# The Hyena inverses of a two-layer diffusion backbone with tokens in the rows, and the filter bias moved into the spectra

## The chip, the cores and the metric

The kernel runs on one core of one Trainium2 chip. The metric is the device time of one execution, in microseconds (us). An execution of the kernel before takes 2646.43 us (median of three). All matrix products read fp32r operands, split into a high and a low half, so that one product of two numbers is made of two or three passes on TensorE.

## The reference

Two layers over 256 latent tokens of width 2048. Layer 0 is a Mamba-2 group beside latent attention, layer 1 an order-2 Hyena long convolution, and each is followed by a SwiGLU FFN. The change lies in layer 1 (`d` is 2048, `gate` is the first and then the second third of the projection, `y` the last third):

```python
def long_conv_bidir(u, h_two):
    seq_len, d = u.shape[1], u.shape[2]
    k = jnp.concatenate([h_two[:, 0], jnp.zeros((1, d)), jnp.flip(h_two[1:, 1], axis=0)], axis=0)
    k = k / jnp.sum(jnp.abs(k), axis=0, keepdims=True)
    kf = jnp.fft.rfft(k, axis=0)
    uf = jnp.fft.rfft(u, n=2 * seq_len, axis=1)
    return jnp.fft.irfft(uf * kf, n=2 * seq_len, axis=1)[:, :seq_len]

# hyena():
proj = dwconv_centred(u @ w_in + b_in, short_w, short_b)
x1, x2, y = proj[..., :d], proj[..., d:2 * d], proj[..., 2 * d:]
for i, gate in enumerate((x1, x2)):
    h_two = jnp.einsum('lf,fkd->lkd', hid, fw_out[:, i]) * window[:, None, :]
    y = gate * (long_conv_bidir(y, h_two) + fbias[i] * y)
return y @ w_out + b_out
```

## The kernel before

**Stages.** A startup stage computes the first layer's modulation by matrix products (`on_pe`, tile `ps_mod`), the sums of squares of both inputs, and the spectra of the Hyena filters (`filters` and `spectra`). Then come layer 0, its output projection, the FFN of layer 0, layer 1 (`layer1`, from about 1446 us to about 1803 us), its output projection, the FFN of layer 1 and a final norm. Activations stand transposed: a row (partition) is a channel, a column a token.

**Weights.** `run` walks over a list of tasks, each with one 1 MB weight block. SP issues the load (`raw`), ScalarE (ACT) writes the high half (`whi`, L339), VectorE (DVE) the low half (`wlo`, L340), TensorE (PE) multiplies: `wide` sends the low weights against 256 columns (L562) and the high weights against 512 (L561, L564). Loads run two tasks ahead and the halves come from a ring of three buffers, so ACT and DVE wait for PE when they are ahead.

**Background steps.** After each task `run` ticks a queue of generators; `hyena_steps(g)` is one of them, for 8 groups `g` of 256 channels, and each runs twice (`o` = 0, 1). The emitted order is then placed by a scheduler for each engine, which fills the spaces between dependent steps with the products of the current task. Every engine works through its own list in order.

**Modulation.** 160 columns of modulation weights are multiplied on DVE (`mods_use`, L445, tile `mraw`), a few for each task at the rates in `MODS` (for layer 0's two parts, the FFN of layer 0, layer 1, the FFN of layer 1).

**Filters.** For each of 8 pieces (4 channel blocks, 2 orders) `filters` loads a weight tile `fwr` by POOL's queue, splits it (`fwh`, `fwl`), makes four products `pss`, multiplies by a window, splits, and sums absolute values in `am`. `spectra` transforms the piece (`psk`), adds and subtracts the two halves (`ko`), writes them to a scratch in HBM (`kscr`), and puts the inverse norm in `kinv`. The tags `fwr`, `fwh` and `fwl` have two buffers each.

**One convolution.** With channels in the rows, `y` is first transposed (`ps_yT`, L1263) so that tokens stand in the rows, even tokens apart from odd ones; it is split, transformed (`ps_u`, 12 products) and multiplied by the spectrum (`kf`). The result is split into `ph` and `pl`. The inverse (`ps_c`) takes `ph` and `pl` as the stationary operand and the inverse table `dih`, `dil` as the moving one, so its result has channels in the rows again: 2 halves of 4 frequency pieces of 3 products, 24 in all, each over 256 columns. Then bias, norm and gate are applied by one ACT and two DVE instructions for each half (L1300 to L1302).

Of the kernel before, what the change touches and what calls it, by code (L numbers as in the profile page):

```python
# [10 lines left out]
F32 = mybir.dt.float32  # L11
F32R = mybir.dt.float32r
AF = mybir.ActivationFunctionType
ALU = mybir.AluOpType
# [3 lines left out]
P = 128  # L18
D = 2048
S = 256  # L20
# [18 lines left out]
MODS = (1.8, 0.6, 0.68, 0.08, 0.6)  # L39
# [132 lines left out]
def _prepare(inputs):  # L172
    g = {k: np.asarray(v) for k, v in inputs.items()}
    f32 = np.float32
    a = {}
# [46 lines left out]
    w = g["ev_w_in"][0]  # L222
# [33 lines left out]
    fw = g["hy_fw_out"][0]  # L256
    a["fw"] = fw.transpose(1, 2, 0, 3).reshape(2, P, 4, 512).transpose(0, 2, 1, 3)
# [9 lines left out]
class _Kernel:  # L267
# [428 lines left out]
    def filters(self, pool):  # L696
        nc, a = self.nc, self.a
# [31 lines left out]
        yield  # L729
        wt = None  # L730
# [39 lines left out]
    def spectra(self, pool, fh, fl, gi, s2, am):  # L770

        nc = self.nc
        g, i = gi // 2, gi % 2
        for w in range(2):
            two = []
            for tt in (1, 0):
                ps = self.ps.tile([P, 512], F32, tag=("acc", "ms")[tt], name=self.nm("psk"), bufs=3)
                r = slice(w * P, (w + 1) * P)
                self.mm3(ps, (fh[:, tt, r], fl[:, tt, r]), (s2[w][0][:, tt], s2[w][1][:, tt]), True, True)
                two.append(ps)  # L780
# [470 lines left out]
    def hyena_steps(self, g):  # L1251
        nc, hp = self.nc, self.hyp
        y = self.hyt[g, 0]
        for o in range(2):
            kf = hp.tile([P, 4, S], F32, tag="kf", name=self.nm("kf"), bufs=1)
            src = self.kscr[2 * (g // 2) + o].rearrange("p (a b) -> p a b", b=512)
            nc.sync.dma_start(kf, src[:, :, (g % 2) * S:(g % 2) * S + S])
            yth = hp.tile([P, 2, S], F32R, tag="yth", name=self.nm("yth"), bufs=1)
            ytl = hp.tile([P, 2, S], F32R, tag="ytl", name=self.nm("ytl"), bufs=1)
            pst = self.ps.tile([P, 2, S], F32, tag="ms", name=self.nm("ps_yT"))  # L1260
            for tt in range(2):
                for c in range(2):
                    nc.tensor.transpose(pst[:, tt, c * P:(c + 1) * P], y[:, c, tt::2], self.mat("ident"))  # L1263
            self.split(yth, ytl, pst)
# [14 lines left out]
            for f2, u in enumerate((ev, odd)):  # L1279
# [10 lines left out]
            if g == 0 and o == 1:  # L1290
                self.mh, self.ml, self.mhl = self.pair("hmix")
            for c in range(2):
                ch = 2 * g + c
                psc = self.ps.tile([P, 512], F32, tag="ms", name=self.nm("ps_c"))
                cs = slice(c * P, (c + 1) * P)
# [7 lines left out]
                if o == 1:  # L1303
                    self.split(self.mh[:, ch, :S], self.ml[:, ch, :S], yc)
# [239 lines left out]
    def layer1(self):  # L1544
        nc, a, hp = self.nc, self.a, self.hyp
        self.hn = {}
# [66 lines left out]
```

## Time and profile before

| | |
|---|---|
| median of three runs | 2646.43 us (2644.79 to 2648.49) |
| the profiled execution | 2648.55 us, span of its instructions 2646.7 us |
| granted TensorE clock, mean of the span | 0.99 of full speed |
| PE busy | 2572.2 us, 97% |
| DVE busy | 2088.8 us, 79% |
| ACT busy | 1428.2 us, 54% |

Times in the rows count from the span's first instruction. A matmul's duration contains its way through the array, and successive ones overlap: what one costs a stream is the distance between two starts. The same holds, to a lesser degree, for DVE.

### The profile page before, as it was taken

What the parts mean: (1) busy time and instruction counts of PE and PEld (TensorE: products, weight loads), DVE (VectorE), ACT (ScalarE), POOL (GpSimd) and SP (SyncE); (2) the same over time, 40 slices, a digit from 0 to 9 for tenths busy, and PEclk for the clock granted to TensorE, in tenths of its full rate; (3) what the DMA queues carried; (4) which work ended last, traced back from release to release, by engine and by line L of the source; (5) the groups of instructions that cost most, each with busy time, mean ns of one, the idle gap of its engine ahead of it and who ended that gap; (6) DMA issues with size and microseconds to landing.
All of it is one profiled execution on the core that took longest, in us unless ns stands there. A gap on an engine that the chain in (4) does not pass through costs nothing.

```text
span 2646.7 us, 39320 instructions
## 1 busy us (share of the span) xinstructions
PE 2572.2 (97%) x15128; PEld 2200.9 (83%) x15128; DVE 2088.8 (79%) x3178; ACT 1428.2 (54%) x2298; POOL 7.4 (0%) x22
## 2 busy tenths in 40 slices
PE   5979999999999999999999999999999999999997
PEld 2548779887988888888888888888998888888886
DVE  7867878777898888888889999898887656656656
ACT  4544656646654544544556755556654544544455
POOL 0000000000000000000000000000000000000000
PEclk9979999999999999999999999999999999999999
DMA  9956557556588887988887555456587654545543
GB/s 354 342 211 221 189 186 278 208 203 234 215 323 310 335 310 284 343 308 298 330 302 271 198 179 180 170 184 235 207 313 261 217 178 169 215 171 195 192 162 125
DMA packets 105610, 635.58 MB, mean 240 GB/s; under 512 B 11344, under 2 KB 19920, under 8 KB 44624
## 3 DMA queue, kind: packets, MB, share of 16 engines
q1 hardware_dynamic: 101904, 620.49, 64.3%
q10 hardware_dynamic: 2304, 8.39, 0.8%
q0 software_dynamic: 1216, 4.20, 0.5%
q8 instruction: 119, 1.95, 0.3%
q14 instruction: 67, 0.55, 0.1%
HBM read 622.55 MB, written 10.49 MB: 239 GB/s over the span
## 4 chain that ended last, share of the span: by engine, by line
PE 92%; DVE 4%; ACT 1%; issue 1%; DMA 1%; SPq 0%; DVEq 0%; ACTq 0%
PE acc L561 41%; PE acc L562 23%; PE acc L819 7%; PE acc L564 3%; PE acc L372 3%; PE acc L373 3%; PE acc L374 3%; PE ps_mod L1383 1%; DVE wlo L340 1%; PE ps_c L372 1%; PE ps_c L374 1%; PE ps_c L373 1%; DVE mraw L445 1%; PE ps_y L1070 0%; PE ps_o L1201 0%
## 5 line engine op out<-in xcount | busy, mean ns | idle before, releaser
L561 PE MATMUL acc<-act,whi 128*128 128x512 f32 x3525 | 1255.6, 396 | 3.9 <-ACT whi L339 3.9
L340 DVE TENSOR_TENSOR wlo<-raw,whi 128x1024 fp32r<-128x1024 f32 (+1 forms) x842 | 938.7, 1119 | 239.1 <-ACT whi L339 232.8
L339 ACT ACTIVATE whi<-raw 128x1024 fp32r<-128x1024 f32 (+1 forms) x842 | 814.6, 972 | 469.7 <-PE acc L561 244.5
L562 PE MATMUL acc<-act,wlo 128*128 128x256 f32 x3760 | 1020.7, 281 | 1.4 <-DVE wlo L340 1.4
L561 PEld LDWEIGHTS acc<-act,whi 128*128 128x128 f32 x3525 | 666.2, 189 | 150.4 <-ACT whi L339 4.9
L562 PEld LDWEIGHTS acc<-act,wlo 128*128 128x128 f32 x3760 | 709.3, 189 | 23.1 <-DVE wlo L340 2.9
L561 PE MATMUL acc<-hh,whi 128*128 128x512 f32 x1280 | 456.4, 395 | 0.0
L445 DVE SCALAR_TENSOR_TENSOR mraw<-mraw,cb 128x2048 f32<-128x2048 f32 x160 | 365.8, 2287 | 30.7 <-DMA mraw<-in_mod 30.4
L562 PE MATMUL acc<-hh,wlo 128*128 128x256 f32 x1408 | 376.2, 282 | 0.0
L561 PEld LDWEIGHTS acc<-hh,whi 128*128 128x128 f32 x1280 | 240.9, 188 | 51.0
L562 PEld LDWEIGHTS acc<-hh,wlo 128*128 128x128 f32 x1408 | 264.7, 188 | 11.5
L571 ACT ACTIVATE sum<-acc 128x256 f32<-128x256 f32 x160 | 61.5, 385 | 271.8 <-PE acc L564 271.8
L372 PE MATMUL acc<-act,whi 128*128 128x258 f32 (+1 forms) x560 | 160.4, 287 | 1.0 <-ACT act L500 1.0
L574 DVE TENSOR_TENSOR sum<-sum,acc 128x256 f32<-128x256 f32 x203 | 85.1, 419 | 96.1 <-ACT sum L571 95.8
L374 PE MATMUL acc<-act,wlo 128*128 128x258 f32 (+1 forms) x560 | 158.4, 284 | 0.9 <-DVE wlo L340 0.9
L373 PE MATMUL acc<-act,whi 128*128 128x258 f32 (+1 forms) x560 | 158.8, 284 | 0.0
L819 PE MATMUL acc<-act,whi 128*128 128x512 f32 x480 | 156.8, 404 | 0.0
L583 ACT ACTIVATE res<-acc,mcol 128x256 f32<-128x256 f32 x144 | 68.2, 474 | 135.5 <-PE acc L564 135.3
L586 DVE SCALAR_TENSOR_TENSOR res<-acc,mcol,res 128x256 f32<-128x256 f32 x160 | 77.1, 483 | 69.2 <-ACT res L583 59.7
L372 PEld LDWEIGHTS acc<-act,whi 128*128 128x128 f32 x560 | 106.6, 191 | 4.0 <-issue 2.5
L374 PEld LDWEIGHTS acc<-act,wlo 128*128 128x128 f32 x560 | 106.4, 190 | 2.0 <-DVE wlo L340 1.1
L373 PEld LDWEIGHTS acc<-act,whi 128*128 128x128 f32 x560 | 106.6, 190 | 1.4 <-issue 0.8
(333 smaller groups left out, 2754.3 us busy)
## 6 DMA issues: line engine op xcount, KB each, us to landing
raw<-in_w SPq DMA_DIRECT2D x176, 1024.0 KB, 4.9
mraw<-in_mod SPq DMA_DIRECT2D x160, 1024.0 KB, 5.1
raw<-in_w SPq DMA_DIRECT2D x128, 704.0 KB, 4.2
raw<-in_hw_in SPq DMA_DIRECT2D x48, 1024.0 KB, 4.8
raw<-in_w_in SPq DMA_DIRECT2D x29, 1024.0 KB, 5.0
mraw<-in_modn SPq DMA_DIRECT2D x19, 1024.0 KB, 9.0
raw<-in_w_o SPq DMA_DIRECT2D x16, 1024.0 KB, 4.8
raw<-in_hw_out SPq DMA_DIRECT2D x16, 1024.0 KB, 4.8
```

Source lines behind the costliest of these rows:

```text
L339: nc.scalar.activation(hi, src, AF.Copy)
L340: nc.vector.tensor_tensor(lo, src, hi.bitcast(F32), ALU.subtract)
L372: t.matmul(out, lh, rh, start=first, stop=False)
L373: t.matmul(out, lh, rl, start=False, stop=False)
L374: t.matmul(out, ll, rh, start=False, stop=last)
L445: self.nc.vector.scalar_tensor_tensor(raw, raw, 1.0, self.cb, ALU.mult, ALU.mult, accum_out=self.mcol[:, j:j + 1])
L561: t.matmul(*high, start=kt == 0, stop=False, skip_group_check=True)
L562: t.matmul(ps[:, :S], wl, x[:, 0], start=False, stop=False, skip_group_check=True)
L564: t.matmul(*high, start=False, stop=True, skip_group_check=True)
L574: nc.vector.tensor_tensor(v, v, halves[0], ALU.add)
L586: nc.vector.scalar_tensor_tensor(v, halves[0], gate, v, ALU.mult, ALU.add)
L819: t.matmul(ps.rearrange("p (a b) -> p a b", a=2), w, self.act[:, j, :, kt, :S], start=kt == 0 and k == 0, stop=kt == n - 1 and k == 2)
```

## The change

With tokens in the rows the inverse is written as a radix-2 step. Sum and difference of the two frequency halves (`ev`, `odd`) are formed on DVE first; the sum serves the even tokens, the difference the odd ones. The table now is the stationary operand (every second of its columns, `tt::2`), and `ph`, `pl` the moving one: 12 products over 256 columns for each convolution instead of 24.

The result has tokens in the rows. Between the two convolutions it stays so: the first gate is transposed to it (`by_tokens`), one DVE product applies the gate, and the second convolution starts from there without a transpose of its own. After the second inverse ACT copies the result to SBUF (`yt`), four transposes (`ps_yC`) turn it back, writing every second column of PSUM, and one DVE product applies the second gate.

The filter bias goes into the spectra: in each piece a row `fb` (bias, repeated over 128 rows, loaded by POOL's queue) is multiplied by the absolute sums `am`, split, and multiplied by a matrix of ones into the sum of even tokens of the first half (`psk`). The inverse norm `kinv` is multiplied into the weights and biases of the short convolution of both gates (four DVE products of 32 columns). `fb` and its halves `fx` share the tags `fwr`, `fwh`, `fwl` with the filter weights.

Two rates in `MODS` change: 0.68 to 0.72 for the FFN of layer 0, 0.08 to 0 for layer 1.

```diff
-MODS = (1.8, 0.6, 0.68, 0.08, 0.6)
+MODS = (1.8, 0.6, 0.72, 0.0, 0.6)
...
+        self.ones_r = pool.tile([P, P], F32R, name="ones_r")
+        nc.scalar.activation(self.ones_r, self.mat("ones"), AF.Copy)
...
     def spectra(self, pool, fh, fl, gi, s2, am):
+        fb = pool.tile([P, 512], F32, tag="fwr", name=self.nm("fb"), bufs=2)
+        nc.gpsimd.dma_start(fb, self.a["fbrow"][gi])
+        nc.vector.tensor_tensor(fb, fb, am, ALU.mult)
+        fx = [pool.tile([P, 512], F32R, tag=t, name=self.nm("fx"), bufs=2) for t in ("fwh", "fwl")]
+        self.split(*fx, fb)
...
-                self.mm3(ps, (fh[:, tt, r], fl[:, tt, r]), (s2[w][0][:, tt], s2[w][1][:, tt]), True, True)
+                self.mm3(ps, (fh[:, tt, r], fl[:, tt, r]), (s2[w][0][:, tt], s2[w][1][:, tt]), True, w == 1 or tt == 1)
+                if w == 0 and tt == 0:
+                    for k in range(2):
+                        nc.tensor.matmul(ps, self.ones_r, fx[k], start=False, stop=k == 1)
...
     def hyena_steps(self, g):
...
+        def by_tokens(v):
             pst = self.ps.tile([P, 2, S], F32, tag="ms", name=self.nm("ps_yT"))
             for tt in range(2):
                 for c in range(2):
-                    nc.tensor.transpose(pst[:, tt, c * P:(c + 1) * P], y[:, c, tt::2], self.mat("ident"))
-            self.split(yth, ytl, pst)
+                    nc.tensor.transpose(pst[:, tt, c * P:(c + 1) * P], v[:, c, tt::2], self.mat("ident"))
+            return pst
+
+        src = by_tokens(self.hyt[g, 0])
...
+            self.split(yth, ytl, src)
...
-                self.split(*[v.rearrange("p (r f) t -> p r f t", f=2)[:, :, f2] for v in (ph, pl)], u)
                 yield
+            t = hp.tile([P, 2, S], F32, tag="t1", name=self.nm("dif"), bufs=2)
+            nc.vector.tensor_tensor(t, ev, odd, ALU.subtract)
+            nc.vector.tensor_tensor(ev, ev, odd, ALU.add)
+            self.split(*parts[0], ev)
+            self.split(*parts[1], t)
...
+            if o == 0:
+                gate = hp.tile([P, 2, S], F32, tag="t1", name=self.nm("gate"), bufs=2)
+                nc.scalar.activation(gate, by_tokens(self.hyt[g, 1]), AF.Copy)
+            psc = self.ps.tile([P, 2, S], F32, tag="ms", name=self.nm("ps_c"))
+            for tt in range(2):
+                for k, r in enumerate((0, 2)):
+                    w = [d[:, r, tt::2] for d in (self.dih, self.dil)]
+                    self.mm3(psc[:, tt], w, (ph[:, r + tt], pl[:, r + tt]), k == 0, k == 1)
+            if o == 0:
+                nc.vector.tensor_tensor(gate, psc, gate, ALU.mult)
+                src = gate
+                continue
+            yt = hp.tile([P, 2, S], F32, tag="t1", name=self.nm("yt"), bufs=2)
+            nc.scalar.activation(yt, psc, AF.Copy)
+            yield
...
-                for f4 in (0, 2, 1, 3):
-                    self.mm3(psc[:, :S], (ph[:, f4, cs], pl[:, f4, cs]), (self.dih[:, f4], self.dil[:, f4]), f4 == 0, f4 == 3)
-                yc = y[:, c, :]
-                t = self.small.tile([P, S], F32, tag="ft", name=self.nm("yt"), bufs=3)
-                nc.scalar.activation(t, yc, AF.Copy, scale=self.col("fbias", o * 16 + ch))
-                nc.vector.scalar_tensor_tensor(t, psc[:, :S], self.kinv[:, o * 16 + ch:o * 16 + ch + 1], t, ALU.mult, ALU.add)
-                nc.vector.tensor_tensor(yc, t, self.hyt[g, 1 + o][:, c, :], ALU.mult)
...
+                for tt in range(2):
+                    nc.tensor.transpose(pst[:, c, tt::2], yt[:, tt, c * P:(c + 1) * P], self.mat("ident"))
+            yc = self.hyt[g, 0]
+            nc.vector.tensor_tensor(yc, pst, self.hyt[g, 2], ALU.mult)
...
     def layer1(self):
+        for v in [self.col("short_w", 48 * k, 32) for k in range(3)] + [self.col("short_b", 0, 32)]:
+            nc.vector.tensor_tensor(v, v, self.kinv, ALU.mult)
```

Two places show what moves in the engines' lists. On PE before, at the end of a second inverse in layer 1 (`acc` are the layer's own products, `ps_c` the inverse, `ps_yT` the next group's transposes):

```order
L373 MATMUL ps_c_14491<-dih,ph_14340 128x256
L374 MATMUL ps_c_14491<-dih,pl_14341 128x256
L562 MATMUL acc_14614<-act,wlo_14427 128x256
L561 MATMUL acc_14614<-act,whi_14426 128x512
...
L1263 MATMUL ps_yT_14512<-mats,hyt_13664 128x128
...
L1263 MATMUL ps_yT_14512<-mats,hyt_13664 128x128 x3
...
L372 MATMUL ps_u_14522<-yth_14510,dfh 128x256
```

And on PE now, at the end of the second inverse of a group (`ps_yC` are the transposes back, `yt` is ACT's copy of `ps_c`):

```order
L375 MATMUL ps_c_14324<-pl_14238,dih 128x256
L376 MATMUL ps_c_14324<-ph_14237,dil 128x256
L564 MATMUL acc_14615<-act,wlo_14439 128x256
L563 MATMUL acc_14615<-act,whi_14438 128x512
...
L1335 MATMUL ps_yC_14339<-mats,yt_14337 128x128 x4
L1273 MATMUL ps_yT_14399<-mats,hyt_13760 128x128 x4
...
L374 MATMUL ps_u_14413<-yth_14406,dfh 128x256
```

The inverse now takes 12 rows of this list, not 24, and behind it stand the transposes back, which wait for ACT's copy of its result; four products of the layer (two of 256 columns, two of 512) lie between.

On POOL before, the loads of the filter stage (`fwr` filter weights, `win` windows):

```order
L735 DMA fwr_227<-in_fw 128x512
L741 DMA win_233<-in_win 128x1024
L735 DMA fwr_347<-in_fw 128x512
L741 DMA win_495<-in_win 128x1024
L735 DMA fwr_489<-in_fw 128x512
L735 DMA fwr_600<-in_fw 128x512
L735 DMA fwr_709<-in_fw 128x512
L741 DMA win_715<-in_win 128x1024
```

And on POOL now:

```order
L739 DMA fwr_229<-in_fw 128x512
L745 DMA win_235<-in_win 128x1024
L739 DMA fwr_349<-in_fw 128x512
L745 DMA win_506<-in_win 128x1024
L780 DMA fb_443<-in_fbrow 128x512
L739 DMA fwr_500<-in_fw 128x512
L745 DMA win_744<-in_win 128x1024
L780 DMA fb_563<-in_fbrow 128x512
L739 DMA fwr_620<-in_fw 128x512
L780 DMA fb_685<-in_fbrow 128x512
```

From the third piece on a load of `fb` stands ahead of each load of `fwr`, and takes one of the two buffers that `fwr` had for itself.

## Rows read from the trace of the kernel before

**Rows 1.** The page, busy time of each engine over the span
```profile
PE 2572.2 (97%) x15128; PEld 2200.9 (83%) x15128; DVE 2088.8 (79%) x3178; ACT 1428.2 (54%) x2298; POOL 7.4 (0%) x22
```

**Rows 2.** The page, the chain that ended last, by engine
```profile
PE 92%; DVE 4%; ACT 1%; issue 1%; DMA 1%; SPq 0%; DVEq 0%; ACTq 0%
```

**Rows 3.** Busy PE, PEld, DVE, ACT, POOL by stretch; clock, DMA share, GB/s
```profile
50.00:104.00 54.00, 51.27 (x270) 27.29 (x270) 47.06 (x96) 27.82 (x52) 2.68 (x5) 1.00 0.93 343
104.00:157.00 53.00, 39.25 (x188) 21.70 (x186) 39.81 (x76) 26.32 (x40) 0.19 (x2) 0.88 0.73 270
...
1100.00:1300.00 200.00, 200.00 (x1139) 174.44 (x1138) 169.60 (x214) 99.48 (x148) 0.00 (x0) 1.00 0.86 318
...
1475.00:1800.00 325.00, 323.36 (x2003) 285.88 (x2001) 302.36 (x525) 188.49 (x298) 0.00 (x0) 1.00 0.52 185
```

**Rows 4.** Timeline of PE: first inverse product, first instruction after the 24
```profile
1701.20 0.28 PE L372 MATMUL ps_c<-dih,ph 128*128 128x256 f32 x1
...
1704.07 0.39 PE L561 MATMUL acc<-act,whi 128*128 128x512 f32 x1
```

**Rows 5.** Timeline of PE: eight transposes and the next instruction
```profile
526.60 1.04 PE L1191 MATMUL ps_pT<-mats,pts 128*128 128x128 f32 x8
527.39 0.48 PE L374 MATMUL acc<-ckv_h,wlo 128*128 128x512 f32 x1
```

**Rows 6.** Weight loads of tile ps_yT (every second column), in ns min/median/max
```profile
L1263 PEld LDWEIGHTS ps_yT<-mats,hyt x64: 194/202/216, 1470.4 to 1787.9; 128*128 128x128 f32 x64
```

**Rows 7.** The same of tile ps_xT (columns that follow each other)
```profile
L1010 PEld LDWEIGHTS ps_xT<-mats,xs x32: 138/140/143, 248.5 to 380.1; 128*128 128x128 f32 x32
```

**Rows 8.** PE's waits, 1430 to 1830 us: total, times, longest
```profile
PE ps_u L372 <- ACT yth L339: 0.4, 1, 0.4
```

**Rows 9.** DVE by line, 1475 to 1800 us: busy, mean ns | idle before, releaser
```profile
L340 DVE TENSOR_TENSOR wlo<-raw,whi 128x1024 fp32r<-128x1024 f32 x87 | 106.4, 1223 | 12.4 <-ACT whi L339 10.0 <-PE acc L562 1.6
...
L1301 DVE SCALAR_TENSOR_TENSOR yt<-ps_c,kinv,yt 128x256 f32<-128x256 f32 x30 | 14.2, 481 | 0.7 <-PE ps_c L374 0.4
L1302 DVE TENSOR_TENSOR hyt<-yt,hyt 128x256 f32<-128x256 f32 x30 | 12.4, 421 | 0.2
...
L340 DVE TENSOR_TENSOR ytl<-ps_yT,yth 128x512 fp32r<-128x512 f32 x16 | 11.0, 687 | 1.4 <-ACT yth L339 1.3
L1277 DVE TENSOR_TENSOR even<-ps_u,odd 128x512 f32<-128x512 f32 x16 | 11.0, 687 | 5.6 <-ACT odd L1275 5.5
...
L445 DVE SCALAR_TENSOR_TENSOR mraw<-mraw,cb 128x2048 f32<-128x2048 f32 x4 | 9.1, 2287 | 0.0
```

**Rows 10.** ACT by line in the same stretch
```profile
L339 ACT ACTIVATE whi<-raw 128x1024 fp32r<-128x1024 f32 x86 | 91.0, 1058 | 73.7 <-PE acc L564 33.9 <-PE acc L561 27.4 <-issue 9.5
...
L1275 ACT ACTIVATE odd<-ps_u 128x512 f32<-128x512 f32 x16 | 9.4, 590 | 8.3 <-PE ps_u L374 8.3
```

**Rows 11.** Timeline of DVE, starts that follow each other
```profile
1785.52 0.48 DVE L1301 SCALAR_TENSOR_TENSOR yt<-ps_c,kinv,yt 128x256 f32<-128x256 f32 x1 [0.40 <-PE ps_c L374]
1785.92 0.47 DVE L1228 SCALAR_TENSOR_TENSOR hyt<-sum,cols,hyt 128x255 f32<-128x255 f32 x1
1786.32 0.42 DVE L1302 TENSOR_TENSOR hyt<-yt,hyt 128x256 f32<-128x256 f32 x1
1786.65 0.48 DVE L1229 SCALAR_TENSOR_TENSOR hyt<-sum,cols,hyt 128x255 f32<-128x255 f32 x1
...
1795.50 0.69 DVE L1281 TENSOR_TENSOR t<-odd,kf 128x512 f32<-128x512 f32 x1
1796.10 0.69 DVE L1282 TENSOR_TENSOR even<-even,kf 128x512 f32<-128x512 f32 x1
```

**Rows 12.** The chain in the startup, 20 to 190 us: start, length
```profile
76.74 0.24 PE psk L373
```

**Rows 13.** DMA traffic from 27 to 157 us
```profile
DMA packets 8886, 41.71 MB, mean 321 GB/s; under 512 B 1024, under 2 KB 1024, under 8 KB 6573
```

**Rows 14.** Loads of tile fwr: POOL's issue in ns, us to landing
```profile
L735 POOL DMA_DIRECT2D fwr<-in_fw x8: 536/536/670, 1.2 to 83.4; - x8
...
DMA to landing us min/median/max: 3.2/5.6/7.0
```

More of the change, by code (lines that the diff above doesn't have):

```diff
@@ L256, in _prepare @@
     fw = g["hy_fw_out"][0]
+    fb = g["hy_fbias"][0].reshape(2, 4, 512).transpose(1, 0, 2).reshape(8, 1, 512)
+    a["fbrow"] = np.broadcast_to(fb, (8, P, 512))
     a["fw"] = fw.transpose(1, 2, 0, 3).reshape(2, P, 4, 512).transpose(0, 2, 1, 3)
@@ L1252, in hyena_steps @@
         nc, hp = self.nc, self.hyp
[L1253 to L1259, printed above, removed]
+        def by_tokens(v):
             pst = self.ps.tile([P, 2, S], F32, tag="ms", name=self.nm("ps_yT"))
@@ L1262, in hyena_steps @@
                 for c in range(2):
-                    nc.tensor.transpose(pst[:, tt, c * P:(c + 1) * P], y[:, c, tt::2], self.mat("ident"))
-            self.split(yth, ytl, pst)
+                    nc.tensor.transpose(pst[:, tt, c * P:(c + 1) * P], v[:, c, tt::2], self.mat("ident"))
+            return pst
+        src = by_tokens(self.hyt[g, 0])
+        for o in range(2):
+            kf = hp.tile([P, 4, S], F32, tag="kf", name=self.nm("kf"), bufs=1)
+            scr = self.kscr[2 * (g // 2) + o].rearrange("p (a b) -> p a b", b=512)
+            nc.sync.dma_start(kf, scr[:, :, (g % 2) * S:(g % 2) * S + S])
+            yth = hp.tile([P, 2, S], F32R, tag="yth", name=self.nm("yth"), bufs=1)
+            ytl = hp.tile([P, 2, S], F32R, tag="ytl", name=self.nm("ytl"), bufs=1)
+            self.split(yth, ytl, src)
             yield from self.wait(1 + HWAITS[0])
@@ L1278, in hyena_steps @@
             nc.vector.tensor_tensor(odd, psu[0], odd, ALU.subtract)
-            for f2, u in enumerate((ev, odd)):
+            both = (ev, odd)
+            parts = [[v.rearrange("p (r f) t -> p r f t", f=2)[:, :, f2] for v in (ph, pl)] for f2 in range(2)]
+            for f2, u in enumerate(both):
                 t = hp.tile([P, 2, S], F32, tag="t1", name=self.nm("t1"), bufs=2)
@@ L1289, in hyena_steps @@
                 yield
-            if g == 0 and o == 1:
+            if o == 0:
[13 more added lines that the diff above has]
+            yield
+            if g == 0:
                 self.mh, self.ml, self.mhl = self.pair("hmix")
+            pst = self.ps.tile([P, 2, S], F32, tag="ms", name=self.nm("ps_yC"))
             for c in range(2):
-                ch = 2 * g + c
-                psc = self.ps.tile([P, 512], F32, tag="ms", name=self.nm("ps_c"))
-                cs = slice(c * P, (c + 1) * P)
-                for f4 in (0, 2, 1, 3):
-                    self.mm3(psc[:, :S], (ph[:, f4, cs], pl[:, f4, cs]), (self.dih[:, f4], self.dil[:, f4]), f4 == 0, f4 == 3)
-                yc = y[:, c, :]
-                t = self.small.tile([P, S], F32, tag="ft", name=self.nm("yt"), bufs=3)
-                nc.scalar.activation(t, yc, AF.Copy, scale=self.col("fbias", o * 16 + ch))
-                nc.vector.scalar_tensor_tensor(t, psc[:, :S], self.kinv[:, o * 16 + ch:o * 16 + ch + 1], t, ALU.mult, ALU.add)
-                nc.vector.tensor_tensor(yc, t, self.hyt[g, 1 + o][:, c, :], ALU.mult)
-                if o == 1:
-                    self.split(self.mh[:, ch, :S], self.ml[:, ch, :S], yc)
+                for tt in range(2):
+                    nc.tensor.transpose(pst[:, c, tt::2], yt[:, tt, c * P:(c + 1) * P], self.mat("ident"))
+            yc = self.hyt[g, 0]
+            nc.vector.tensor_tensor(yc, pst, self.hyt[g, 2], ALU.mult)
+            for c in range(2):
+                self.split(self.mh[:, 2 * g + c, :S], self.ml[:, 2 * g + c, :S], yc[:, c])
             yield from self.wait(1 + HWAITS[2])
```

## The prediction

> **What bounds the kernel now.** I read the page first: PE is busy for 97% of the span, DVE for 79%, ACT for 54% [rows 1], and 92% of the chain that ended last lies on PE [rows 2]. So time is saved where PE's list gets shorter, as long as the next engine follows. Then I read busy times by stretch, because the average hides where that is in doubt [rows 3]. In the FFN of layer 0 DVE is busy 169.6 of 200 us. In layer 1 (1475 to 1800 us) PE is busy 323.4 of 325 us and DVE 302.4, or 93.0%: the second engine is only 22.6 us behind the first. In the startup (50 to 157 us) neither is full: first PE leads with 51.3 of 54 us, later both stand at 39 to 40 of 53 us, which is the picture of a chain that changes engines.
>
> A matmul's own duration says little, since they overlap. I took costs from distances between starts.
>
> **The change, part by part.**
>
> *Inverse products.* 24 of them take from 1701.20 to 1704.07 us, 2.87 us or 0.1196 us each [rows 4]. The moving operand has 256 columns before and after, so I keep this price. 16 convolutions lose 12 products each: 192 x 0.1196 = -23.0 us on PE.
>
> *Transposes.* 64 before; now 4 at the start of a group, 4 for the first gate and 4 back, 96. Eight transposes of plain columns take 0.79 us, 0.099 each [rows 5]: 32 x 0.099 = +3.2 us. Those back write every second column of PSUM, which no row shows. If it doubles them, the term is 6.3 us; a gain has no reason, since the columns are as many. I take 3.2, the value of the row.
>
> *Weights with a step of two.* The remaining 192 products load every second column of the table. The two kinds of transposes bound this: a load of every second column lasts 202 ns [rows 6], of neighbours 140 ns [rows 7], a difference of 62 ns. If the load stays hidden behind the product before it, it costs 0; if each product is late by the whole difference, 192 x 0.062 = 11.9 us. I take 0, because loads here run beside products.
>
> A rule of the Trainium skill bears on both points. In "SBUF — State Buffer", section "Door 1: The DMA port swizzle (why `[64,N]` ≈ `[32,N]`)", it says that SBUF is read in lines of 16 bytes and that two hits in a line give full speed, so that a step of two fp32 values is free; but PSUM has lines of 8 bytes, and "any non-contiguous PSUM access pattern significantly slows down matmuls". Rows 6 and 7 do not bear out the first half for the load's own duration, and the measurement decides; the second half speaks against the transposes back, and by it their term is nearer 6.3 than 3.2. No run here shows that yet.
>
> *DVE in layer 1.* Successive starts give its prices [rows 11]: a product of 256 columns out of PSUM with scalar 0.40, a plain one of 256 0.34, one of 512 0.60 us. Removed are 32 pairs, 32 x (0.40 + 0.34) = -23.7. Added are, in each convolution, the difference and the sum, and one product with the gate: 48 x 0.60 = +28.8. The rate of 0 in layer 1 takes 4 modulation columns out of the stretch, 4 x 2.29 = -9.2 [rows 9]. Net -4.1: DVE needs 302.4 - 4.1 = 298.3 us.
>
> *Does DVE keep up?* PE alone would need 323.4 - 23.0 + 3.2 = 303.6 us. DVE's 22.6 idle us are of two kinds. 12.4 us lie ahead of the low weight halves [rows 9], behind ACT, which itself waits 61.3 us for PE to give buffers back [rows 10]: that is slack, and goes when PE gets faster. The other 10.2 us are delays in the chain (the largest is DVE waiting for ACT's copy `odd`, 5.5 us) and stay. 298.3 + 10.2 = 308.5 us: DVE then sets the pace, 4.9 us behind what PE could do. So the stretch shrinks from 325.0 to 308.5, by 16.5 us. Its bounds: 303.6 plus PE's present 1.6 of idle (-19.8), and DVE at no more than its present 93.0%, 298.3 / 0.930 = 320.7 (-4.3). I take 16.5, since the idle time named has a cause in each row.
>
> *A new wait on PE.* The transposes back wait for ACT's copy of 512 columns, whose like takes 0.59 us [rows 10], behind four products worth about 0.7 us; in the last group nothing lies between. What is queued behind them on PE is the layer's next products, whose weight halves then come free later. The nearest like wait (`ps_u` for the split of `ps_yT`, with as many products between) cost PE 0.4 us in all 16 cases [rows 8]. I take 2 us for eight; at most, with ACT caught in a weight split of 1.06 us each time, 8 x 0.9 = 7.
>
> ACT itself loses 32 copies of 256 columns and gains 16 of 512, at 58% load [rows 3]: nothing. Layer 0's FFN gets six modulation columns more, 6 x 2.29 = 13.7 us of DVE in a stage where 200 us alone leave it 30 us idle [rows 3]; nothing, and nothing is gained by it but the room in layer 1. If that cover failed it would cost 13.7. The product of `kinv` with 32 columns, four times, is under 1 us.
>
> *Startup.* Each of 8 pieces adds two DVE instructions of 0.60 us, one ACT copy, two PE products of 0.24 [rows 12], and a load of 256 KB: DVE 9.6, PE 3.8 us, 2.1 MB of DMA, which at 321 GB/s [rows 13] would be 6.5 us of a DMA that is 93% busy in the first half [rows 3]. Everything in the pieces must end before layer 0's activations can be written, so this stage is on the path. About five pieces fall in the half that PE leads (5 x 0.48 = 2.4) and three in the half where the chain changes to DVE (3 x 1.2 = 3.6): +6.0 us. Bounds: 0, if the pauses take it up, and 9.6 + 3.8 = 13.4, if all is in series.
>
> *Sum.* -16.5 + 2 + 6 = -8.5 us. The profiled execution took 2648.55 us (span 2646.7), 2.1 more than the median of 2646.43; the difference is applied to the median: **2638 us**, 0.3% faster. The extreme bounds are -19.8 + 0 + 0 and, for this path, -4.3 + 7 + 13.4.
>
> **Rivals.**
>
> *DVE holds its share.* If DVE cannot run above 93% in layer 1, the stretch gives only 4.3 us back and the startup takes them: -4.3 + 2 + 6 = +3.7, 2650 us, no change. For it: DVE works its list in order and stands at 93% already, and a convolution's DVE work grows. Against it: half of its idle time is slack.
>
> *The startup hides its additions*, and PE sets layer 1: -19.8 + 2 + 0 = -17.8, 2629 us. For it: DVE is idle 13 of 53 us in the second half of the startup [rows 3]. Against it: those pauses are links of the chain.
>
> *Loads with a step of two set the pace.* +11.9 on the forecast: +3.4, 2650 us, no change. The Trainium skill, "TensorE: Matmul & The Clock Gate", section "Back-to-back issue gap", says that in a stream of loads and products the spacing is set by both. No run here shows a stepped load in a stream of 256-column products.
>
> *The filter stage runs out of weights.* `fb` takes one of the two buffers of `fwr`, and POOL issues each `fwr` behind an `fb` that waits for the previous one's split. If a piece's load then starts only when the piece should, each of the last 7 pieces loses an issue and a landing, 0.54 + 5.6 us [rows 14], 43 us in all: -8.5 + 43 = +34, 2681 us, slower. It decides from about 2 us for each piece ((8.5 + 5.3) / 7). Against it: a piece lasts about 130 / 8 = 16 us, and the load can start when the previous split is done, early in the piece before.
>
> **How the numbers follow.** 0.2% of this kernel, 5.3 us, is what a measurement can tell from no change. Forecast 0.47, with its own range 2632 to 2645; DVE holds its share 0.20; startup hidden 0.15; stepped loads 0.08; filter stage 0.10. Faster: nearly all of the forecast (0.40), all of the hidden startup, and a twentieth from the edges: 0.60. No change: the rest of the forecast, most of the two cases at 2650: 0.25. Slower: the filter stage and the far edge of those two: 0.15. Range: from 2627, under the hidden startup, to 2652, over the two cases of no change, which leaves out the filter stage and the ends.
>
> **What would show it.** In the changed profile: `ps_c` 192 products at 0.12 us from start to start (right) or 0.18 (stepped loads); `ps_yC` at 0.10 or 0.20; layer 1's stretch some 16 us shorter with DVE above 95% busy and PE at 98 or 99% (forecast), or DVE at 93% and PE waiting for `wlo`; the first product of layer 0 about 6 us later; PE's waits for `yt` about 2 us; no wait of ACT for the load of `fwr`. The forecast is wrong if layer 1 shrinks by less than 10 us, or the startup grows by over 13.

## The result and the profile after

The changed kernel takes 2666.07 us (median of six runs, 2661.48 to 2671.51) against 2646.72 us, a ratio of 1.0077 with an interval of 1.0066 to 1.0089: 0.8% slower. Forecast were 2638 us, 0.3% faster. The profiled execution took 2663.69 us, with a span of 2661.9 us, 15.2 more than before; the medians are 19.4 apart, and the table below accounts for the 15.2 alone.

The page's busy times, and the chain that ended last by engine, answer to [rows 1, 2]:

```profile
PE 2572.6 (97%) x14984; PEld 2189.8 (82%) x14984; DVE 2101.6 (79%) x3182; ACT 1428.1 (54%) x2291; POOL 11.7 (0%) x30
...
PE 87%; DVE 7%; DMA 3%; issue 2%; ACT 1%; SPq 0%; DVEq 0%; ACTq 0%; POOLq 0%
```

PE has 144 instructions fewer and the same busy time; 5% of the chain has moved from PE to DVE and DMA. Where the 15.2 us lie is read from the starts of two tiles, the products `acc` and DVE's residuals `res` (160 of them, 16 for each output projection and 64 for each FFN). The last two columns are experiments told below, *e4* and *e10*:

| us in the profiled execution | before | after | new layer 1, old rates | old layer 1, new rates |
|---|---|---|---|---|
| to the first product of layer 0 | 171.5 | 188.8 | 190.9 | 169.2 |
| to the end of layer 0's FFN | 1275.1 | 1274.8 | 1275.7 | 1276.9 |
| layer 1, to the 4th residual behind it | 374.4 | 370.8 | 380.7 | 372.0 |
| to the 16th residual | 70.0 | 70.2 | 70.1 | 68.9 |
| FFN of layer 1, to its first residual | 135.6 | 139.8 | 135.5 | 144.9 |
| the rest | 620.1 | 617.5 | 620.5 | 617.8 |

The startup costs 17.3 us where 6 were forecast, and layer 1 gives 3.6 where 14.5 were. The rest adds 1.5. Not every row repeats equally well: nine profiled executions without the filter part reach the first product after 168.6 to 172.3 us, while the row of layer 1 is 374.3 to 374.4 us in three executions of the old layer and 368.2 to 371.3 in eight of the new one.

**Prices.** Timeline of PE after (start, length): eight transposes, then an inverse. They answer to [rows 4, 5].

```profile
1780.27 0.66 PE L1335 MATMUL ps_yC<-mats,yt 128*128 128x128 f32 x4
1780.77 0.64 PE L1273 MATMUL ps_yT<-mats,hyt 128*128 128x128 f32 x4
1781.16 0.48 PE L563 MATMUL acc<-act,whi 128*128 128x512 f32 x1
...
1796.85 0.28 PE L375 MATMUL ps_c<-pl,dih 128*128 128x256 f32 x1
...
1798.17 0.28 PE L564 MATMUL acc<-act,wlo 128*128 128x256 f32 x1
```

Eleven products, from 1796.85 to 1798.17, are 0.120 us each, as before: weights with a step of two cost the stream nothing. Four transposes that write every second column of PSUM take 0.50 us, 0.125 each, beside 0.0975 for those that follow (seven groups of four give 0.49 or 0.50). The forecast's prices on PE hold, but for 0.9 us.

**Layer 1.** Busy PE, PEld, DVE, ACT, POOL in the startup and in layer 1 after, with clock, DMA share and GB/s; they answer to [rows 3]:

```profile
50.00:104.00 54.00, 45.62 (x229) 24.51 (x227) 42.81 (x85) 25.25 (x46) 4.29 (x8) 0.97 0.90 325
104.00:157.00 53.00, 44.11 (x202) 25.83 (x200) 45.89 (x89) 29.92 (x48) 3.22 (x6) 0.90 0.68 243
...
1494.00:1812.00 318.00, 311.68 (x1865) 269.45 (x1864) 297.79 (x501) 181.66 (x277) 0.00 (x0) 1.00 0.51 176
1812.00:1824.00 12.00, 9.17 (x33) 7.58 (x34) 6.28 (x12) 5.00 (x9) 0.00 (x0) 0.57 0.30 102
```

The stretch from 1494 to 1812 us has the same 87 weight splits `wlo` as the 325 us of [rows 3]. DVE stands at 297.79 of 318 us in it, 93.6%, where the forecast wanted over 95%. DVE by line in that stretch answers to [rows 9] (busy, mean ns | idle before, releaser):

```profile
L342 DVE TENSOR_TENSOR wlo<-raw,whi 128x1024 fp32r<-128x1024 f32 x87 | 105.7, 1219 | 10.9 <-ACT whi L341 10.7
L1296 DVE TENSOR_TENSOR even<-ps_u,odd 128x512 f32<-128x512 f32 x16 | 11.0, 685 | 1.1 <-ACT odd L1294 0.8
L1308 DVE TENSOR_TENSOR dif<-even,odd 128x512 f32<-128x512 f32 x16 | 10.9, 683 | 0.0
L1309 DVE TENSOR_TENSOR even<-even,odd 128x512 f32<-128x512 f32 x16 | 10.9, 683 | 0.0
L1324 DVE TENSOR_TENSOR gate<-ps_c,gate 128x512 f32<-128x512 f32 x8 | 5.5, 685 | 4.4 <-ACT gate L1317 4.4
```

The idle time ahead of `wlo`, which I called slack, is still there (12.4 before, 10.9 now). The wait for `odd`, which I called fixed, has gone from 5.5 to 0.8, and a new one of 4.4 us for the gate's copy has come. The other side is PE's waits, 1440 to 1840 us (total, times, longest), 9.6 us with a last one of 0.3, in place of the single 0.4 of [rows 8]:

```profile
PE acc L564 <- DVE wlo L342: 4.2, 8, 1.0
PE acc L563 <- DVE act L342: 2.4, 2, 1.7
PE ps_c L374 <- ACT ph L341: 2.0, 2, 1.8
PE ps_yC L1335 <- ACT yt L1328: 0.7, 1, 0.7
```

The layer's end shows it best. The short convolution of the layer's last weight block starts on ACT 339.3 us after layer 0's FFN, 16.7 us earlier than before (356.0). But the first residual behind the layer comes only 5.0 us earlier (358.4 against 363.4): DVE still has the whole last convolution ahead of it. Busy time tells the same. Busy PE, PEld, DVE, ACT, POOL from layer 0's last residual, first before, then after, each in two parts: to that short convolution, and from there to the first residual behind the layer:

```profile
1446.60:1802.60 356.00, 354.33 (x2241) 315.86 (x2240) 331.93 (x582) 211.35 (x341) 0.00 (x0) 1.00 0.51 183
1802.60:1810.00 7.40, 7.40 (x44) 6.20 (x44) 6.37 (x12) 5.73 (x9) 0.00 (x0) 1.00 0.75 283
```
```profile
1463.60:1802.90 339.30, 334.02 (x2051) 291.76 (x2050) 318.67 (x547) 203.93 (x320) 0.00 (x0) 1.00 0.51 178
1802.90:1822.00 19.10, 14.50 (x70) 12.12 (x69) 13.36 (x23) 6.23 (x12) 0.00 (x0) 0.76 0.31 113
```

Over both parts DVE has 6.3 us less work (332.0 against 338.3) and as much idle time as before (26.4 against 25.1), and the layer is 5.0 us shorter. In the second part DVE still works for 13.4 us, where 6.4 were left before: 7.0 us of the shorter first part are work put off. PE's timeline at the end, with the wait in brackets:

```profile
1809.95 0.28 PE L564 MATMUL acc<-act,wlo 128*128 128x256 f32 x1
1812.05 0.39 PE L374 MATMUL ps_c<-ph,dih 128*128 128x256 f32 x1 [1.82 <-ACT ph L341]
...
1814.74 0.41 PE L375 MATMUL ps_c<-pl,dih 128*128 128x256 f32 x1
1814.96 0.41 PE L376 MATMUL ps_c<-ph,dil 128*128 128x256 f32 x1
1816.12 1.12 PE L1335 MATMUL ps_yC<-mats,yt 128*128 128x128 f32 x4 [0.75 <-ACT yt L1328]
1818.93 0.79 PE L563 MATMUL acc<-act,whi 128*128 128x512 f32 x1 [1.69 <-DVE act L342]
```

PE runs out of products at 1810, waits four times (1.82, 0.34, 0.75 and 1.69 us), and works at a mean granted clock of 0.57 from 1812 to 1824 us (the last line of the stretches above): products stand 0.21 us apart in place of 0.12.

**Startup.** POOL's queue after (start, length, what the issue waited for):

```profile
12.00 0.54 POOL L739 DMA_DIRECT2D fwr<-in_fw  x1 [5.18 <-DVE sin L686]
54.46 0.53 POOL L745 DMA_DIRECT2D win<-in_win  x1 [41.92 <-DVE sv L759]
62.06 0.54 POOL L780 DMA_DIRECT2D fb<-in_fbrow  x1 [7.07 <-ACT row L1421]
...
89.77 0.54 POOL L780 DMA_DIRECT2D fb<-in_fbrow  x1 [3.32 <-ACT fwh L341]
```

The load of a piece's bias row stands in order behind `win`, and needs a buffer of the ring that it shares with `fwr`. The chain that ended last holds two landings in full, and DVE (start, length, wait) is held by the second:

```profile
62.06 5.05 DMA fb<-in_fbrow
...
89.77 8.05 DMA fb<-in_fbrow
```
```profile
97.91 0.69 DVE L781 TENSOR_TENSOR fb<-fb,am 128x512 f32<-128x512 f32 x1 [4.21 <-DMA fb<-in_fbrow]
98.52 1.28 DVE L759 TENSOR_TENSOR sv<-pss,win 128x512 f32<-128x512 f32 x2
```

Behind `fb` stands `sv`, for which PE waits:

```profile
99.25 0.63 PE L374 MATMUL pss<-fwh,hs 128*128 128x512 f32 x1 [3.28 <-DVE sv L759]
99.68 0.63 PE L375 MATMUL pss<-fwl,hs 128*128 128x512 f32 x1
```

Its products are then 0.43 us apart, against 0.23 before the wait.

### The profile page after: what moved, and what is told of

Same layout as the page of the kernel before. It is cut to its first block, busy times and chain, and to the rows that moved or that the text cites. A ratio compares the mean times of both kernels' runs of the same rounds, so it can differ in the third digit from the quotient of the medians.

```text
span 2661.9 us, 39024 instructions
## 1 busy us (share of the span) xinstructions
PE 2572.6 (97%) x14984; PEld 2189.8 (82%) x14984; DVE 2101.6 (79%) x3182; ACT 1428.1 (54%) x2291; POOL 11.7 (0%) x30
## 4 chain that ended last, share of the span: by engine, by line
PE 87%; DVE 7%; DMA 3%; issue 2%; ACT 1%; SPq 0%; DVEq 0%; ACTq 0%; POOLq 0%
PE acc L563 38%; PE acc L564 21%; PE acc L832 7%; PE acc L566 3%; PE acc L374 3%; PE acc L375 3%; PE acc L376 3%; DVE wlo L342 2%; PE ps_mod L1418 1%; DMA raw<-in_w 1%; DMA mraw<-in_mod 1%; DMA fb<-in_fbrow 0%; ACT whi L341 0%; PE ps_y L1083 0%; PE ps_o L1214 0%
## 5 line engine op out<-in xcount | busy, mean ns | idle before, releaser
L564 PEld LDWEIGHTS acc<-act,wlo 128*128 128x128 f32 x3760 | 710.1, 189 | 31.8 <-DVE wlo L342 11.3
```

Source lines behind the costliest of these rows:

```text
L564: t.matmul(ps[:, :S], wl, x[:, 0], start=False, stop=False, skip_group_check=True)
```

## Experiments

Medians; ratios and intervals are against the kernel before on the same chip. 0.2% is 5.3 us. The edits are shortened: `...` and words behind a `#` stand for what is left out.

**The two halves of the change apart.** *e1*: the kernel before with the filter part.

```diff
 (before) spectra:
+        fb = pool.tile([P, 512], F32, tag="fwr", ...)   # and its load, product, split
+                        nc.tensor.matmul(ps, self.ones_r, fx[k], ...)
```

> The kernel before with the filter-bias part in the spectra alone (rows loaded, multiplied by am, split, two products with ones); layer 1 is the one before and still adds its own bias, so the bias counts twice. Theory (the startup loses what the trace of after shows there, +17.3 us at the first acc product): +17 us against before, about 2664, range 2660 to 2668. Rival (the startup part costs what was forecast, +6, and most of the loss is made in layer 1): about 2653, range 2649 to 2656.

2668.01 us, 1.0078 (1.0064 to 1.0092), as the theory had it. The first product of layer 0 comes at 188.2 us, +16.7.

*e2*: the changed kernel with those lines taken out.

> The changed kernel without the filter-bias part (no rows of bias, no products with ones; the bias is left out of the output). New layer 1, kinv folded into the short filter, new rates of loads. Theory (VectorE sets the pace of layer 1 at the busy share it had, so 23 us less of products bring only what VectorE has less): 5 to 7 us faster than before, about 2641, range 2638 to 2644. Rival (layer 1 gives the forecast 14.5 us by itself, and the late start takes part of it in the whole kernel): about 2632, range 2629 to 2636.

2646.85 us, 1.0002 (0.9993 to 1.0011). The whole loss is the filter part's, and the rest of the change gives nothing that can be measured: less than either theory had. In its profiled execution layer 1 gives the same 3.6 us as in the changed kernel, and the first part of FFN 1 takes 5.8 back. *e4* looks at the rates of the modulation columns:

```diff
-MODS = (1.8, 0.6, 0.72, 0.0, 0.6)
+MODS = (1.8, 0.6, 0.68, 0.08, 0.6)
```

> The changed kernel with the modulation rates of before (0.68 and 0.08 in place of 0.72 and 0.0). Theory (the rates only move 1.3 us pieces of VectorE work between stages): within 2 us of the changed kernel, 2664 to 2669. Rival (the rates are what costs layer 1's gain, or what holds it up): 4 us or more away, to either side.

2674.41 us, 1.0100 (1.0087 to 1.0114), 8.3 more than the changed kernel: my theory falls (and a column takes 2.29 us of DVE, not the 1.3 that I wrote there). By the table layer 1 takes 9.9 us more for 9.2 us of DVE (four columns of 2.29), and the new inverse alone makes the layer 6.3 us *longer* than before. *e10* is the same edit turned round, on the kernel before.

> The kernel before with nothing but the new rates of modulation columns (0.72 and 0.0 in place of 0.68 and 0.08). Theory (before, TensorE is full in layer 1, so four columns of VectorE less there bring at most its 1.6 us of idle time; the next FFN pays for some columns and gets some back): within 2 us of before, 2645 to 2648. Rival (VectorE set the pace of layer 1 before as well, and the rates alone give what they gave with the new inverse): 8 to 10 us faster, about 2638.

2650.75 us, 1.0016 (1.0007 to 1.0025): neither theory, 4 us more. With the old inverse the rates bring 2.4 us in layer 1 and cost 9.3 in the first part of the next FFN, where DVE now waits for columns that land late (stretch 1885 to 2032 us; 1.1 us, once, before):

```profile
DVE mraw L445 <- DMA mraw<-in_mod: 7.7, 7, 2.4
```

PE, which waited for nothing there before, now waits 2.6 us for weight halves, and its granted clock is 0.90 from 1922 to 1956 us. That the columns cause this is argued from the order of events, not shown.

**What sets layer 1's pace.** Both start from e2. *e6* takes away DVE work, *e7* PE work.

```diff
 (e6)
-                nc.vector.tensor_tensor(u, u, kf[:, f2]..., ALU.mult)
 (e7)
-                    self.mm3(psc[:, tt], w, (ph[:, r + tt], pl[:, r + tt]), k == 0, k == 1)
+                    nc.tensor.matmul(psc[:, tt], w[0], ph[:, r + tt], ...)
+                    nc.tensor.matmul(psc[:, tt], w[0], pl[:, r + tt], ...)
```

> The new layer 1 without the filter bias in the spectra, and in each convolution without the two products of the spectrum's real part on VectorE (32 instructions of 0.60 us, 19.2 us less VectorE; that part of the computation is left out). TensorE's work stays. Theory (VectorE sets layer 1's pace, up to the few us that TensorE still waits): 10 to 16 us faster than the new layer 1 with all its VectorE work, about 2634, range 2630 to 2638. Rival (TensorE, its stepped weights or the transposes set the pace): within 3 us of it, 2643 to 2648.

> The new layer 1 without the filter bias in the spectra, and with two products in place of three in each of the inverse's steps (the low half of the table is left out: 64 products of 0.12 us, 7.7 us less TensorE). VectorE's work stays. Theory (VectorE sets the pace): within 2 us of the new layer 1 as it is, 2645 to 2648. Rival (TensorE sets it): 6 to 8 us faster, about 2640.

e6: 2634.62 us, 0.9959 (0.9947 to 0.9972), 12.2 less than e2. e7: 2646.17 us, 1.0004 (0.9995 to 1.0013), 0.7 less. Taking 7.7 us from PE brings nothing. Busy PE, PEld, DVE, ACT, POOL from 1475 to 1800 us, of e2, of e6 and of e7:

```profile
1475.00:1800.00 325.00, 315.83 (x1883) 272.85 (x1882) 299.78 (x506) 183.78 (x280) 0.00 (x0) 0.99 0.50 174
```
```profile
1475.00:1800.00 325.00, 322.23 (x1947) 281.91 (x1947) 292.58 (x490) 192.69 (x296) 0.00 (x0) 1.00 0.52 180
```
```profile
1475.00:1800.00 325.00, 311.11 (x1832) 268.10 (x1830) 301.71 (x510) 185.83 (x284) 0.00 (x0) 0.99 0.50 174
```

With less DVE work PE fills up to 322 us, which is why 19.2 us give only 12; with less PE work PE just idles more. But e6 also shortens the chain of dependent steps in each convolution. To part work from chain, *e16* (on e2) and *e17* (on the kernel before) add two DVE instructions in each convolution:

```diff
             self.split(yth, ytl, src)
+            spare = self.mats[:, 4 * P:8 * P]
+            for _ in range(2):
+                nc.vector.tensor_tensor(spare, spare, spare, ALU.mult)
```

> The new layer 1 (no filter bias in the spectra), with two more VectorE instructions of 0.60 us in each convolution, 19.2 us in all, on a constant that nobody reads any more, placed where the convolution is with TensorE. Theory (VectorE's work as such sets layer 1's pace, at some 93%): 15 to 20 us more than the new layer 1 without them, about 2664, range 2660 to 2668. Rival (the length of each convolution's chain sets it, and VectorE's idle time is slack): at most 6 us more, 2647 to 2653.

> The kernel before, with the same 32 instructions (19.2 us of VectorE that nobody waits for) at the same place of its convolutions. As the prediction had it, 12.4 of VectorE's 22.6 idle us in layer 1 are slack: 7 us more than before, about 2653, range 2650 to 2656. Rival (VectorE holds 93% whatever happens, and sets the pace before as well): 15 to 21 us more, about 2664. Third (TensorE sets the pace before, and all of it is hidden): 2646 to 2649.

2645.39 us, 0.9992 (0.9983 to 1.0001), and 2643.85 us, 0.9991 (0.9982 to 1.0000): nothing, which looked like the end of my theory. But the experiment did not do what it was meant to. DVE's instructions on `mats` in e16, with first and last start:

```profile
L1274 DVE TENSOR_TENSOR mats<-mats x32: 678/688/693, 246.1 to 398.0; 128x512 f32<-128x512 f32 x32
```

They have no operand of layer 1 and run in layer 0. *e18* and *e19* give them one:

```diff
-                nc.vector.tensor_tensor(spare, spare, spare, ALU.mult)
+                nc.vector.tensor_tensor(spare, kf[:, :2], yth.bitcast(F32), ALU.mult)
```

> The new layer 1 (no filter bias in the spectra) with two more VectorE instructions of 0.60 us in each convolution, 19.2 us in all, products of its spectrum and its split tile into a constant that nobody reads any more. Theory (VectorE's work as such sets layer 1's pace): 15 to 20 us more than without them, about 2664, range 2660 to 2668. Rival (the length of each convolution's chain sets it, and VectorE's idle time is slack): at most 6 us more, 2645 to 2653.

> The kernel before with the same 32 instructions in its convolutions. As the prediction had it, 12.4 of VectorE's 22.6 idle us in layer 1 are slack: 7 us more than before, about 2653, range 2650 to 2657. Rival (VectorE holds 93% whatever happens): 15 to 21 us more, about 2664. Third (TensorE alone sets the pace before): 2645 to 2649.

In e18 they now lie in layer 1, and nobody waits for them:

```profile
L1274 DVE TENSOR_TENSOR mats<-kf,yth x32: 679/684/693, 1485.4 to 1802.3; 128x512 f32<-128x512 f32 x32
```

e18: 2666.61 us, 1.0077 (1.0064 to 1.0091), 19.8 us more than e2 for 19.2 us of work. e19: 2655.53 us, 1.0038 (1.0026 to 1.0051), 9.7 more than before. Busy PE, PEld, DVE, ACT, POOL from layer 0's last residual to the first behind layer 1, of e18 and of e19:

```profile
1447.00:1822.20 375.20, 354.03 (x2118) 308.28 (x2117) 351.49 (x601) 211.20 (x331) 0.00 (x0) 0.97 0.47 167
```
```profile
1443.60:1813.70 370.10, 362.76 (x2283) 323.62 (x2282) 355.66 (x624) 217.79 (x348) 0.00 (x0) 1.00 0.52 183
```

In e18 that stretch is 17.3 us longer than in e2 (357.9), and DVE still idles 23.7 us in it. In e19 it is 6.7 longer than before (363.4), DVE's idle time falls from 25.1 to 14.4, and DVE is 96% busy. So DVE's work sets the pace of the new layer 1, nearly one for one, while 9.5 to 12.5 us of it fitted into the idle time of the old one. The added instructions also stand in DVE's list ahead of their convolution's next step, so that a longer chain has a share in the 17.3 us is not excluded; at the same place in the old layer they cost 6.7.

**The startup.** *e3*: the bias rows in a constant's room, loaded behind the filter weights of the same step; the halves `fx` in buffers of their own (one each). To make room, the tiles `am1` and `odd` move into the same constant.

```diff
             nc.gpsimd.dma_start(fwr, a["fw"][i, g])
+            fb = self.cb[:, (gi % 2) * 512:(gi % 2 + 1) * 512]
+            nc.gpsimd.dma_start(fb, a["fbrow"][gi])
...
-        fx = [pool.tile([P, 512], F32R, tag=t, ..., bufs=2) for t in ("fwh", "fwl")]
+        fx = [pool.tile([P, 512], F32R, tag=t, ..., bufs=1) for t in ("fxh", "fxl")]
```

> The changed kernel, whole, with the bias rows in buffers of their own (a constant that is loaded only after the startup lends the room), their loads issued right behind the filter weights of the same step, and the split halves in buffers of their own: the two weights' rings are as before. Same bytes, same work. Theory (the rows come late: their load stands behind a full ring and the window's load in GpSimd's queue, and VectorE waits in order): the startup comes back to +6 or +7 (VectorE 9.6 us and TensorE 3.8 us more work, of which a part is hidden), so 2655, range 2651 to 2659. Rival (the added work and 2.1 MB of bytes on a full startup cost it, wherever the load is issued): 2664 to 2667.

2659.98 us, 1.0054 (1.0041 to 1.0066): 6.1 us come back, where I had expected 7 to 15. Whether the rows' place in the queue or their buffer did it was not tried apart. The first stretch of the startup is that of before again, and DVE no longer waits for `fb`:

```profile
50.00:104.00 54.00, 52.51 (x274) 26.86 (x276) 48.69 (x100) 28.38 (x53) 3.75 (x7) 1.00 0.87 326
```

Against e2, the same kernel without the filter part, 13.1 us are left. Three cuts in e3 ask where: *e9* loads one row in place of eight (and writes every product to one buffer), *e14* makes product and split in the first piece alone, *e15* leaves out the products with ones.

```diff
 (e9)
+            if gi == 0:
+                nc.gpsimd.dma_start(self.cb[:, :512], a["fbrow"][gi])
 (e14)
+        if gi == 0:   # product with am and split; later pieces use its halves
 (e15)
-                        nc.tensor.matmul(ps, self.ones_r, fx[k], start=False, stop=k == 1)
```

> The whole change with the bias rows early and in buffers of their own, but only the first of the eight is loaded (0.26 in place of 2.1 MB; the other pieces use the first one's rows, so the bias is another). VectorE's, ScalarE's and TensorE's added work is all there. Theory (what the early rows left of the loss, some 10 us in the startup, is the added work itself, of which nearly all is on the path): within 2 us of the early rows with all loads, 2658 to 2662. Rival (the loss that is left is bytes: 1.8 MB at 321 GB/s): 5 to 6 us less, about 2654.

> The whole change with the early rows; the product with am and the split are made in the first of the eight pieces alone, and all pieces use its halves (so the bias is another). All loads and all 16 products with ones stay. It takes 14 VectorE instructions (8.4 us) and 7 ScalarE copies out of the startup. Theory (VectorE's additions, and with them the chain from am to the products, are most of the 10 to 12 us that the startup still loses): 6 to 9 us less than the early rows alone, about 2653, range 2651 to 2655. Rival (they lie in the pauses; TensorE and bytes make the loss): 2657 to 2661.

> The whole change with the early rows, without the 16 products with ones (the bias is left out of the output); loads, products with am and splits stay, but nobody waits for them. Theory (TensorE's additions cost their own 3.8 us at most, VectorE's work stays on the path): 2 to 4 us less than the early rows alone, about 2657. Rival (what costs is that the products wait for the chain am, product, split): 7 us or more less, 2653 or under.

e9: 2656.75 us, 1.0050 (1.0036 to 1.0064), 3.2 less than e3, between the two theories. e14: 2648.67 us, 1.0008 (0.9999 to 1.0017), 11.3 less, more than the theory had. e15: 2658.10 us, 1.0042 (1.0030 to 1.0055), 1.9 less. The three cuts sum to 16.4 us, more than the 13.1, so they overlap; the part of DVE and ACT is by far the largest, and not because the products wait for it: in e15 nobody does.

**GpSimd for VectorE.** If DVE is short, an idle engine might take some. *e8* is e3 with layer 1's two sums there, *e11* is e3 with the bias product and the low split there (and the two halves of each spectrum in the other order), *e12* has both, *e13* both with the rates of before.

```diff
 (e8)
-            nc.vector.tensor_tensor(t, ev, odd, ALU.subtract)
-            nc.vector.tensor_tensor(ev, ev, odd, ALU.add)
+            nc.gpsimd.tensor_tensor(t, ev, odd, ALU.subtract)
+            nc.gpsimd.tensor_tensor(ev, ev, odd, ALU.add)
 (e11)
-        nc.vector.tensor_tensor(fb, fb, am, ALU.mult)
+        nc.gpsimd.tensor_tensor(fb, fb, am, ALU.mult)
```

> The whole change with the bias rows early and in buffers of their own, and in layer 1 the difference and the sum of each convolution on GpSimd in place of VectorE (32 instructions, 19.2 us less VectorE; nothing is left out). Theory (VectorE sets layer 1's pace, and GpSimd, idle there, takes the two without holding VectorE up): 10 to 14 us less than the early rows alone, about 2648, range 2645 to 2651. Rival (GpSimd is so slow on 512 columns, or holds VectorE up so, that the longer chain of each convolution eats it): no gain or a loss, 2658 to 2675.

> The whole change with the early rows, and in the startup the bias product and the split's low half on GpSimd (16 instructions, 9.6 us less VectorE), the real part's products last in each piece so that they wait less. Layer 1 as in the change. Theory (of the 10 us that are left in the startup the larger part is VectorE's 9.6, in series): 5 to 9 us less than the early rows alone, about 2653, range 2650 to 2656. Rival (what is left is TensorE's, the bytes and the chain, whichever engine multiplies): 2658 to 2662.

> Both of these: the sums of layer 1 and the bias product and low split of the startup on GpSimd, the early rows. Theory (the two add, as they lie in different stages): 2641, range 2637 to 2646, faster than before by 0.2%. Rival (GpSimd costs in either place what VectorE saves): 2655 or more.

> The same with the modulation rates of before (0.68 and 0.08). Theory (with VectorE relieved in layer 1 it no longer sets the pace there, so four columns more cost it little, and FFN1 starts with fewer columns left, which was worth 4 to 9 us there): 0 to 5 us less than the one with the new rates, about 2638. Rival (VectorE still sets layer 1's pace, and the columns cost 8 us as they did): 2648.

All four theories fall. e8: 2697.03 us, 1.0195 (1.0181 to 1.0209), 37.1 *more* than e3, beyond its rival's range too. e11: 2661.21 us, 1.0062 (1.0048 to 1.0076), 1.2 more. e12: 2699.70 us, 1.0207 (1.0193 to 1.0221). e13: 2702.70 us, 1.0219 (1.0205 to 1.0233). POOL by line in e8, and what PE waits for, 1440 to 1880 us:

```profile
L1308 POOL TENSOR_TENSOR dif<-even,odd 128x512 f32<-128x512 f32 x16 | 39.5, 2467 | 1026.1 <-DVE odd L1305 1026.1
L1309 POOL TENSOR_TENSOR even<-even,odd 128x512 f32<-128x512 f32 x16 | 21.6, 1350 | 1.3
```
```profile
PE ps_c L374 <- ACT ph L341: 26.7, 11, 3.3
```

2.47 and 1.35 us in place of 0.60 each make the chain of a convolution 2.6 us longer, 42 us in 16, beside the 35.4 by which e8's layer exceeds e3's (393.8 against 358.4 us to the first residual). So chain length seems to count too, when it grows that much; no run parts it from DVE's own loss, since DVE is busy for 328.8 us there, only 3.3 less than in e3. No version here that computes the whole result beats the kernel before; the new layer 1 alone equals it, but lacks the bias.

## Why the prediction was wrong

*Prices on PE, right.* Products and stepped loads cost what was forecast, transposes back 0.9 us more in all 32. The Trainium skill's rule on PSUM ("SBUF — State Buffer", "Door 1: The DMA port swizzle (why `[64,N]` ≈ `[32,N]`)") shows as 0.125 against 0.0975 us for a transpose: nearer no cost than its "significantly". What the Trainium skill's "TensorE: Matmul & The Clock Gate", section "Back-to-back issue gap", says, that loads and products set the spacing together, did not make itself felt here: with stepped loads of 195 ns the products stayed 0.120 us apart. The wait for ACT's copy, put at 2 us, is 0.7 on PE.

*"Does DVE keep up?", the step that failed in layer 1.* The 298.3 us of DVE work were right (297.8 measured, in a stretch of 318). Wrong was to add only 10.2 us of idle time and to call the 12.4 ahead of `wlo` slack that goes when PE gets faster. In the kernel before it was slack, as the prediction had it: e19 fits 9.5 of its 19.2 us into the whole kernel, 12.5 by the layer's own stretch. But that is so because PE set the pace there (busy 354.3 of 356.0 us up to the last weight block). With PE faster DVE becomes the one that is waited for. Its idle time from layer 0's last residual to the first behind layer 1 did not shrink (25.1 before, 26.4 after), and e18's instructions took up only some 2 us of it. The rival "DVE holds its share" gave -4.3 for the stretch (-2.3 with the wait), and -3.6 came. Its reason also fits the sign of the inverse: with the old rates the new inverse makes the layer 6.3 us longer (e4), for it trades 20 us of PE, which then no longer sets the pace, for 5 us of DVE, which does (48 x 0.60 against 32 pairs of 0.74).

*The stretch was taken for the layer.* Up to its last weight block layer 1 did shrink by 16.7 us, beside a forecast of 16.5. That agreement is luck: DVE's idle time up to there fell by 3.4 us (from 24.1 to 20.6), not by 12.4, and 7.0 us of the gain are DVE work put off to the end. I ended the sum there; the last convolution, which before lay beside the last products, now stands behind them, and 11.7 us go back.

*The rates, wrong.* "Nothing is gained by it but the room in layer 1" missed the next stage: FFN 1's first part is 4.2 us longer after, 9.3 in e10, with DVE waiting for columns. The term of 0 should have been some +4, of which 2.6 come back at the end. The count was off too: layer 0's FFN got five columns more, not six, and FFN 1's first part 16 in place of 15.

*Startup, wrong by its size.* +6 was forecast, with 13.4 as the bound if all were in series. Of the 19.2 us by which the whole kernel exceeds e2, 6.1 are the late rows (e3) and 13.1 the added work and bytes (e14, e9, e15): about the bound. I had split the pieces between a PE half and a DVE half and charged each only the leader's part; e14 says that the additions on DVE and ACT cost 11.3 us, for 8.4 us of DVE instructions. The rival "runs out of weights" had the right place, POOL's queue and the shared ring, with the wrong price: not an issue and a landing in each of seven pieces (43 us), but two landings that show.

What stays open: why DVE, which reaches 96% in e19, cannot fill the last 6% of the new layer 1. The idle time ahead of `wlo` in the layer is 11.8 us after (12.6 before) and falls to 8.5 in e18, to 6.8 in e19; that it belongs to the loop in which ACT's split waits for PE and PE for DVE's is argued, not shown. And moving the bias product and the low split to POOL took 9.6 us from DVE without a gain; whether POOL's slowness or ACT's wait for it ate that was not tried.

## What to carry over

When the second engine is busy for over 90% of a stage and works in order, its idle time can be slack only as long as the first engine sets the pace; an edit that trades the first engine's work for the second's should, from the point where the pace changes hands, be charged the second's work in full. Take a stage's gain where the next stage starts, with the last chain behind the last bulk work, not at the end of the bulk. A small load that shares a ring of buffers and a queue can come as late as the slowest thing ahead of it there.

## What the hardware showed that I had not expected

GpSimd took 2.47 us for a 128x512 fp32 subtraction and 1.35 for an addition (median of the first 2.52, from 1.30 to 3.27), where VectorE takes 0.68. VectorE itself slowed beside it: in e8 the split of `dif` took 1047 ns in the mean (686 in the changed kernel), and the first step of the short filter 597 (477).

```profile
L342 DVE TENSOR_TENSOR pl<-dif,ph 128x512 fp32r<-128x512 f32 x15 | 15.7, 1047 | 12.3 <-ACT ph L341 12.3
```

TensorE's pauses were paid twice: after waits of 1.82 and 3.28 us its products stood 0.21 and 0.43 us apart in place of 0.12 and 0.23. The mean granted clock was 0.57 from 1812 to 1824 us and 0.54 from 99.25 to 102 us, near the lower of its two levels (1.2 of 2.4 GHz).
